# HGRN2's value projection in wide tiles with its heads turned on VectorE, the start and the layers' seams in another order: a four-layer decoder trunk on one core

## The chip, the core and the metric

One Trainium2 chip, one of its cores. The metric is device time in microseconds (us) of one execution. PE is TensorE, with PEld its weight loads; DVE is VectorE, ACT ScalarE, POOL GpSimd, and SP the engine whose queue issues nearly all DMAs here. The whole trunk runs as one program.

## What is computed

x is 1024 positions by 1024 channels in fp32. Four layers follow one another: HGRN2, sliding-window attention (SWA), gated DeltaNet (GDN), HGRN2 again.

```python
for i in range(DEPTH):                                  # 4
    mod = (c @ ada_w[i] + ada_b[i])[:, None, :]
    shift, scale, gate = jnp.split(mod, 3, axis=-1)
    h = rmsnorm(x, norm_g[i]) * (1.0 + scale) + shift
    y = mixer_i(h, ...)                                 # i % 3: 0 HGRN2, 1 SWA, 2 GDN
    x = x + gate * y

def hgrn2_mixer(h, w_in, w_out, onorm_g, lb):           # 8 heads, dk = dv = 128, chunks of 64
    q, f_pre, i_, z = jnp.split(h @ w_in, 4, axis=-1)   # w_in 1024 x 4096
    log_f = jnp.log(lb + (1.0 - lb) * jax.nn.sigmoid(f_pre))
    k = (1.0 - lb) * jax.nn.sigmoid(-f_pre)
    o = hgrn2_scan(silu(q), k, i_, log_f)               # S = exp(b_last) S + k^T v, o = A v + q exp(b) S
    return (rmsnorm(o, onorm_g) * jax.nn.silu(z)) @ w_out
```

SWA has 16 query heads over 4 key heads of width 64, rotary angles and a norm of q and k, a window of 128. GDN has 8 key heads and 16 value heads of width 128, a short convolution on q, k and v, and a triangular solve per chunk of 64.

## The kernel before

**Layout.** Positions are cut into two halves of HT = 512 (`hf`), each of NC = 4 groups of 128; channels into KT = 8 groups of 128. x is kept with channels on partitions, one SBUF slot per half (`xslot`, two). The normed input of a layer is kept as a pair `hhi`, `hlo` in fp32r (`hslot`, four), every weight as `w_hi`, `w_lo`; a product is `mm3`, three matmuls hi·hi, lo·hi, hi·lo, one PSUM tile over eight channel groups (24 matmuls). `load_w` (L170-186) brings a piece of weights by DMA, rounds it on ACT and takes the remainder on DVE; three raw and four rounded pieces are held.

**Kinds of projection.** `proj_fm` has weights standing and 512 positions streaming (PSUM tile `proj_ps`); `proj_tm` has positions standing and 256 weight columns streaming (`projt_ps`); HGRN2's values, two heads at a time, and all of SWA's q, k and v use `proj_tm`.

**The mixers.** In HGRN2, `mix` takes one head, half by half: products inside blocks of 32 at three levels (`lev_ps`, L1040, and L1087 for the last one, of 96, 64 and 32 columns on three column groups of PE), the transposed keys (`kh_ps`), the output and state matmuls (`o_ps`, `s_ps`), the norm of the output (L1132), its transpose on PE (`ot_ps`, L1136), the gate's multiply on DVE (L1139), and a store to `od` in DRAM (L1141), from where the output projection reads it (`out_load`, `out_mm`; PSUM tile `outp_ps`). Head 7 skips the store. Values lie in `hg_v`, three buffers. In GDN, `conv` empties a projection's PSUM tile on ACT (L644, L648), sums the taps on DVE (L650); `inverse` solves the triangular systems with groups of tiny matmuls (`z_ps`); `scan` carries the state. Outputs of GDN are turned by a transpose of 32x32 blocks on DVE (L859) and four stores.

**What sets the order.** `weave` draws from several generators (a head's mixing, the next heads' projections, the next layer's conditioning `side`) by their yielded costs, and a scheduler places each engine's instructions by priority (`high_priority`); then every engine, and SP's queue too, runs its own list strictly in that order. `tied` keeps a group of matmuls together. A layer's first projections are drawn early (`early`), beside the end of the one before.

**The seams.** After each half of a layer is added to x, `norm` takes the statistics and `norm_apply` writes hhi and hlo of the next layer, eight pieces, each of DVE (L504), ACT (L505), DVE (L506). For SWA and GDN x is spilled to `xd` in DRAM, as its slots are needed.

**The start.** x comes in eight tiles and is transposed on PE; `ada_first` builds the first layer's shift and scale, four parts of 2 MB of `ada_w`, all as rows on PE (`ada_row`, L400), then turned into columns (`ada_ps`, L449). `AO` lists the order of these and of two preloaded weight columns. The first projection follows.

Of the kernel before, what the change touches and what calls it, by code (L numbers as in the profile page):

```python
# [20 lines left out]
P = 128  # L21
T = 1024
# [8 lines left out]
NB = {"n_acc": 1, "n_sq": 2, "n_t": 2}  # L31
# [4 lines left out]
EO, EW, EV = 60, 150, 300  # L36
# [8 lines left out]
AO = ((2, True), (0, True), 0, D, (3, True), (1, True))  # L45

ZL = ((2, 0, 1),), ((3, 0, 1),), ((4, 0, 1),), ((5, 0, 1),), ((6, 0),), ((6, 1),), ((7, 0, 1),), ()
# [36 lines left out]
class Trunk:  # L84
    def __init__(self, ctx, tc, ins):
# [11 lines left out]
        self.od = [self.dram.tile([D * (1 + n), T], F32, name=f"od{n}") for n in range(2)]  # L97
        self.zd = self.dram.tile([2 * D, T], F32, name="zd")
        self.hhi, self.hlo = [None, None], [None, None]
        self.x = [None, None]  # L100
        self.oo, self.pre = {}, {}
# [12 lines left out]
    def early(self, g, pe=0):  # L114

        self.pw, self.pe = EW, pe
        with self.tc.high_priority(offset=EO):
            drain(g)
        self.pw = self.pe = 0
# [25 lines left out]

    def psum(self, tag, name, bufs):
        return self.ps.tile([P, HT], F32, name=name, tag=tag, bufs=bufs)
# [18 lines left out]
    def load_w(self, src, scale=None):  # L166

        nc = self.nc
        shape = list(src.shape)
        raw = self.wp.tile([P, HT], F32, name="w_raw", tag="raw", bufs=RAW)  # L170
        hi = self.wp.tile([P, HT], F32R, name="w_hi", tag="whi", bufs=WB)
        lo = self.wp.tile([P, HT], F32R, name="w_lo", tag="wlo", bufs=WB)
# [22 lines left out]

    def preload(self, w, cols):

        w = w.rearrange("(k p) n -> p k n", p=P)
        self.pre.update((c0, self.load_cols(w, c0)) for c0 in cols)

    def mm3(self, out, a, b, start, stop):
# [4 lines left out]
        mm(out, a[1], b[0], start=False, stop=stop)  # L206
# [87 lines left out]
    def load_x(self, sp, hf):  # L294

        nc = self.nc
        x = self.ins["x"].rearrange("o t d -> (o t) d")
# [3 lines left out]
        for c in range(NC):  # L301
            tt, ts = hf * NC + c, slice(c * P, (c + 1) * P)
            xt = sp.tile([P, D], F32, name="x_in", tag="x_in", bufs=3)
            nc.sync.dma_start(xt, x[tt * P:(tt + 1) * P, :])
            sq = sp.tile([P, D], F32, name="x_sq", tag="x_sq", bufs=1)
            nc.scalar.activation(sq, xt, AF.Square, accum_out=ssq[:, c:c + 1])
            for g in range(2):
# [5 lines left out]
                (nc.scalar.copy if n % 2 else nc.vector.tensor_copy)(dst, src)  # L313
# [3 lines left out]
    def store_x(self, out, hf):  # L317

        nc = self.nc
        o = out.rearrange("o t d -> (o t) d")  # L320
        with self.tc.tile_pool(name=f"out{hf}", bufs=1, reuse_waits="tile", side="right") as op:
            for g in range(2):
                for c in range(NC):
                    t0 = (hf * NC + c) * P
                    xo = op.tile([P, HT], F32, name="x_out", tag="x_out", bufs=5)
                    pt = self.proj_ps("xo_ps")
                    for k in range(4):
                        nc.tensor.transpose(pt[:, k * P:(k + 1) * P], self.x[hf][:, 4 * g + k, c * P:(c + 1) * P], self.ident)
                    (nc.scalar.copy if c % 2 else nc.vector.tensor_copy)(xo, pt)
                    nc.sync.dma_start(o[t0:t0 + P, g * HT:(g + 1) * HT], xo)  # L330
# [57 lines left out]
    def ada_first(self, i, sp, steps):  # L388

        nc = self.nc  # L390
        w = self.ins["ada_w"][i].rearrange("(k p) n -> p k n", p=P)
        for part, pe in steps:
            wk = self.hslot("ada_w0").bitcast(F32)
            for g in range(2):
                nc.sync.dma_start(wk[:, 4 * g:4 * g + 4, :], w[:, 4 * g:4 * g + 4, part * HT:(part + 1) * HT])
            acc = sp.tile([P, HT], F32, name="ada_acc", tag="acc", bufs=2)
            if pe:
                pr = self.psum("lev", "ada_row", 2)
                for k in range(KT):
                    nc.tensor.matmul(pr[0:1, :], self.cT[:, k:k + 1], wk[:, k, :], start=k == 0, stop=k == KT - 1)  # L400
                acc = acc[0:1, :]
                nc.scalar.copy(acc, pr[0:1, :])
            else:
                for k in range(KT):
                    self.ada_step(acc, wk[:, k, :], k)
            self.ada_cols(i, part, acc)
# [59 lines left out]
    def norm(self, i, hf):  # L466
        self.norm_apply(i, hf, self.norm_stats(hf))

# [27 lines left out]
    def norm_apply(self, i, hf, rb):  # L496
        nc = self.nc
# [3 lines left out]
        for k in range(KT):  # L501
            t = self.np.tile([P, HT], F32, name="n_t", tag="n_t", bufs=NB["n_t"])
            G, S = self.gcol[:, i, k:k + 1], self.shift(i, k)
            nc.vector.scalar_tensor_tensor(t, x[:, k, :], G, rb, ALU.mult, ALU.mult)  # L504
            nc.scalar.activation(hhi[:, k, :], t, AF.Identity, bias=S)  # L505
            nc.vector.scalar_tensor_tensor(hlo[:, k, :], t, S, hhi[:, k, :].bitcast(F32), ALU.add, ALU.subtract)  # L506

# [29 lines left out]
    def gdn(self, i, side):  # L537
# [98 lines left out]
        def conv(dd, hf, ps, ct, out):  # L636
# [7 lines left out]
            nc.scalar.copy(xs[:, 3:], ps)  # L644
# [4 lines left out]
            for j in (2, 1, 0):  # L649
                nc.vector.scalar_tensor_tensor(y, xs[:, j:j + HT], w(j), y, ALU.mult, ALU.add)  # L650
# [81 lines left out]
        def inverse(u, dd):  # L732
# [75 lines left out]
            with self.burst():  # L808
                for g in range(N):
                    for z, p_, b_ in ((za, 0, 1), (zb, 2, 3)):  # L810
                        nc.tensor.matmul(z[R[b_], g, :], uv[R[p_], g, R[b_]], Tc[R[p_], g, :], start=True, stop=True)
# [4 lines left out]
            yield 900  # L816
            za, zb = bank("z_ps", 32), bank("z_ps", 32)
            self.tied([f for g in range(N) for f in (
# [6 lines left out]
            yield 1300  # L825
# [666 lines left out]
```

## Time and profile before

| What | Value |
|---|---|
| Time, median of 3 runs | 2690.08 us (2689.09 to 2697.81) |
| Profiled execution, its own time | 2695.95 us |
| Its span | 2694.2 us, mean granted clock 0.992 |
| First projection's matmul | at 55.11 us |
| HGRN2 of layer 0, SWA, GDN, HGRN2 of layer 3 end | about 630, 1110, 2100, 2690 us |
| Matmuls on PE, as recorded | 18,927 (a matmul with fp32 operands is recorded twice, for its two passes) |

A row of a timeline has the start, the duration, engine, line, operation, tiles (out<-in), shape and count; in brackets the idle time ahead of it and what ended it. PE's durations overlap, since matmuls are pipelined, so steps are read from start to start. A row of waits has who waited on whom, the total in us, how often, and the longest. A row of costly groups has busy us and mean ns of one after the bar. A row of DMA issues has the size of one and the median us from issue to landing.

### The profile page before, as it was taken

The numbers are of one execution on the slowest core, as the hardware profiler recorded it, in microseconds if no ns is written. First come the engines' busy times: TensorE is split into PE (matmuls) and PEld (weight loads), VectorE is DVE, ScalarE is ACT, GpSimd is POOL, SyncE is SP. The second block draws the span as 40 slices with busy tenths as digits, with TensorE's granted clock in tenths as the row PEclk, the third lists the DMA queues.
The fourth block names the chain that finished last, engine by engine and source line by source line (L and its number), as shares of the span: only waits on it lengthen the run. The fifth ranks groups of instructions, "written<-read, shape, count | busy, mean of one in ns | idle before, by whom it ended". The sixth has DMA issues, their size and how long they took to land.

```text
span 2694.2 us, 51458 instructions
## 1 busy us (share of the span) xinstructions
PE 2609.7 (97%) x18927; PEld 2102.4 (78%) x18927; DVE 2010.2 (75%) x5619; ACT 1272.9 (47%) x3268; POOL 136.7 (5%) x352
## 2 busy tenths in 40 slices
PE   8999999999999999999999999999999999999998
PEld 4878878778878777677877777777788878787877
DVE  6776766788687877777988888989876766656575
ACT  4333333444454655454556556666644433333342
POOL 0000100000000000001001101100000000000000
PEclk9999999999999999999999999999999999999999
DMA  6332222344223252333343333333584221111133
GB/s 241 92 93 84 68 79 72 110 137 157 59 87 103 75 158 91 114 98 84 102 115 99 96 105 100 94 97 82 179 254 132 71 60 37 56 51 43 49 118 115
DMA packets 361490, 273.29 MB, mean 101 GB/s; under 512 B 70499, under 2 KB 294166, under 8 KB 361238
## 3 DMA queue, kind: packets, MB, share of 16 engines
q1 hardware_dynamic: 360950, 268.96, 33.9%
q8 instruction: 149, 2.44, 0.4%
q14 instruction: 103, 0.84, 0.1%
q0 software_dynamic: 288, 1.05, 0.1%
HBM read 224.77 MB, written 45.15 MB: 100 GB/s over the span
## 4 chain that ended last, share of the span: by engine, by line
PE 71%; DVE 17%; DMA 5%; ACT 3%; issue 3%; SPq 1%; POOL 0%; DVEq 0%; ACTq 0%; POOLq 0%
PE proj_ps L206 10%; PE proj_ps L205 9%; PE proj_ps L204 9%; PE outp_ps L204 5%; PE outp_ps L205 5%; PE outp_ps L206 5%; DMA ada_w<-in_ada_w_dram 3%; PE projt_ps L204 3%; PE projt_ps L206 3%; PE projt_ps L205 3%; DVE w_lo L180 2%; DVE gd_tb L650 2%; PE pv_ps L1374 1%; DVE ada_acc L413 1%; PE w_ps L890 1%
## 5 line engine op out<-in xcount | busy, mean ns | idle before, releaser
L204 PE MATMUL proj_ps<-hhi,w_hi 128*128 128x512 f32 x1664 | 675.8, 406 | 6.1 <-ACT gd_tb L648 5.9
L206 PE MATMUL proj_ps<-hhi,w_lo 128*128 128x512 f32 x1664 | 679.9, 409 | 0.0
L205 PE MATMUL proj_ps<-hlo,w_hi 128*128 128x512 f32 x1664 | 671.2, 403 | 0.0
L204 PEld LDWEIGHTS proj_ps<-hhi,w_hi 128*128 128x128 f32 x1664 | 315.3, 190 | 59.4 <-ACT gd_tb L648 6.3
L205 PEld LDWEIGHTS proj_ps<-hlo,w_hi 128*128 128x128 f32 x1664 | 314.7, 189 | 59.0 <-issue 2.4
L206 PEld LDWEIGHTS proj_ps<-hhi,w_lo 128*128 128x128 f32 x1664 | 315.0, 189 | 56.1 <-issue 1.0
L179 ACT CAST w_hi<-w_raw 128x512 fp32r<-128x512 f32 x332 | 202.0, 611 | 303.3 <-PE proj_ps L205 188.1
L180 DVE TENSOR_TENSOR w_lo<-w_raw,w_hi 128x512 fp32r<-128x512 f32 x332 | 223.1, 674 | 155.2 <-ACT w_hi L179 129.1
L205 PE MATMUL projt_ps<-w_lo,hhi 128*128 128x256 f32 x896 | 258.7, 291 | 4.7 <-DVE w_lo L180 4.7
L204 PE MATMUL projt_ps<-w_hi,hhi 128*128 128x256 f32 x896 | 257.8, 290 | 0.6 <-ACT w_hi L179 0.6
L206 PE MATMUL projt_ps<-w_hi,hlo 128*128 128x256 f32 x896 | 256.8, 290 | 0.0
L204 PE MATMUL outp_ps<-o_hi,w_hi 128*128 128x512 f32 x576 | 229.2, 400 | 4.7 <-ACT o_hi L1200 3.4
L205 PE MATMUL outp_ps<-o_lo,w_hi 128*128 128x512 f32 x576 | 229.4, 399 | 0.0
L206 PE MATMUL outp_ps<-o_hi,w_lo 128*128 128x512 f32 x576 | 226.8, 396 | 0.7 <-DVE w_lo L183 0.7
L205 PEld LDWEIGHTS projt_ps<-w_lo,hhi 128*128 128x128 f32 x896 | 171.1, 192 | 8.1 <-DVE w_lo L180 6.0
L204 PEld LDWEIGHTS projt_ps<-w_hi,hhi 128*128 128x128 f32 x896 | 171.1, 192 | 3.7 <-ACT w_hi L179 1.0
L206 PEld LDWEIGHTS projt_ps<-w_hi,hlo 128*128 128x128 f32 x896 | 170.8, 192 | 2.4 <-issue 1.0
L650 DVE SCALAR_TENSOR_TENSOR gd_tb<-gd_xs,taps,gd_tb 128x512 f32<-128x512 f32 x192 | 145.2, 756 | 28.3 <-ACT gd_tb L648 19.7
L182 ACT ACTIVATE w_hi<-w_raw,par 128x512 fp32r<-128x512 f32 (+1 forms) x136 | 94.3, 698 | 137.0 <-PE outp_ps L205 89.2
L204 PEld LDWEIGHTS outp_ps<-o_hi,w_hi 128*128 128x128 f32 x576 | 108.8, 189 | 29.1 <-ACT o_hi L1200 4.9
L413 DVE SCALAR_TENSOR_TENSOR ada_acc<-ada_w,par,ada_acc 128x512 f32<-128x512 f32 x140 | 104.8, 749 | 33.4 <-DMA ada_w<-in_ada_w_dram 32.5
L206 PEld LDWEIGHTS outp_ps<-o_hi,w_lo 128*128 128x128 f32 x576 | 108.7, 189 | 23.5 <-DVE w_lo L183 1.3
(398 smaller groups left out, 4894.8 us busy)
## 6 DMA issues: line engine op xcount, KB each, us to landing
ada_w<-in_ada_w_dram SPq DMA_DIRECT2D x160, 256.0 KB, 2.8
w_raw<-in_hg_in_w_dram SPq DMA_DIRECT2D x136, 256.0 KB, 2.8
w_raw<-in_gd_in_w_dram SPq DMA_DIRECT2D x108, 256.0 KB, 3.0
o_in<-od SPq DMA_DIRECT2D x72, 256.0 KB, 3.2
w_raw<-in_gd_out_w_dram SPq DMA_DIRECT2D x64, 256.0 KB, 2.9
w_raw<-in_sw_in_w_dram SPq DMA_DIRECT2D x48, 256.0 KB, 2.9
w_raw<-in_hg_out_w_dram SPq DMA_DIRECT2D x40, 256.0 KB, 2.8
ada_w<-in_ada_w_dram SPq DMA_DIRECT2D x8, 1024.0 KB, 9.2
```

The lines of the kernel that those rows point to most:

```text
L179: nc.scalar.copy(hi, raw)
L180: nc.vector.tensor_tensor(lo, raw, hi.bitcast(F32), ALU.subtract)
L182: nc.scalar.activation(hi, raw, AF.Copy, scale=scale)
L204: mm(out, a[0], b[0], start=start, stop=False)
L205: mm(out, a[0], b[1], start=False, stop=False)
L206: mm(out, a[1], b[0], start=False, stop=stop)
L413: self.nc.vector.scalar_tensor_tensor(acc, w, c, acc, ALU.mult, ALU.add)
L650: nc.vector.scalar_tensor_tensor(y, xs[:, j:j + HT], w(j), y, ALU.mult, ALU.add)
L890: nc.tensor.matmul(po[:, hd[a]], dd["u"][a, hf][:, cs], rhs, start=True, stop=True)
L1374: nc.tensor.matmul(po[a * 64:(a + 1) * 64], vg[:, n + 1 - nkb + b, :], p4[:, :, a, :], start=b == 0, stop=b == nkb - 1)
```

## The change

It has eight parts; the names are those of the code after.

1. *Wide values.* HGRN2's values are projected 512 columns at a time (`proj_wide`, PSUM tile `projw_ps`), four heads at once, over all eight groups of positions. They lie in the two slots of x, head 7's apart (`v7`); so x is spilled in HGRN2 layers too, and comes back (`fill_x`) ahead of the output projection. From head 1 on z of a head is projected while it is mixed.
2. *Heads 0 to 6 turned on DVE.* The normed output is transposed in blocks of 32x32 on DVE (L1192), stored in four pieces to a scratch `pd` in DRAM (L1195), read back while the next half is mixed (L1074), multiplied by the gate on DVE (L1075) and stored to `od` (L1076).
3. *The last level* is 16 matmuls of 32, 64, 64 and 32 columns on four column groups, tied.
4. *GDN.* The z groups are issued behind the last product (`apart`) and their yields are larger; two more units' gate projections are drawn early.
5. *Norm.* `norm_apply` is a generator, its scratch is in PSUM (`n_t` in the "lev" banks); the second half is drawn inside the next layer, in GDN within `conv`, behind the tap sums (`self.last`, `hold`, `piece`).
6. *SWA.* V and Q are projected first, K after them, with one rsqrt per two tiles; the matmuls of P·V are tied.
7. *Start.* All of `ada_w` is asked for at once, behind half of x; parts 2 and 3 are rows on PE, parts 0 and 1 sums on DVE; the second half of x is copied on ACT alone; tables of angles and taps come last.
8. *The store* of x uses a free slot of hhi instead of a pool of its own.

```diff
+    def apart(self, mms):
+        with self.tc.issue_after(self.mm.ins):
+            self.tied(mms)
...
+        row(2)
+        steps(0)
+        row(3)
+        self.ada_cols(i, 0, acc[0])
+        steps(1)
+        self.ada_cols(i, 1, acc[1])
...
-            t = self.np.tile([P, HT], F32, name="n_t", tag="n_t", bufs=NB["n_t"])
+            t = self.psum("lev", "n_t", 2)
...
-            nc.scalar.copy(xs[:, 3:], ps)
+            with self.tc.issue_after(self.hold.ins) if self.hold else nullcontext():
+                nc.scalar.copy(xs[:, 3:], ps)
...
+            self.piece = None
+            with self.tc.issue_after(last.ins):
+                drain(take(self.last, self.parts))
+            self.hold = self.piece
...
-        self.early(proj_kq(0, ds[0], ((0,),)), EV)
+        self.parts = 4
+        self.early(chain(proj_kq(0, ds[0], ((0,),)), proj_z(1, ds[1], (0,)), proj_z(2, ds[2], (0,))), EV)
+        drain(self.last)
...
+        def gate():
+            h, hf, z = pend.pop()
+            rows = (slice(h * P, (h + 1) * P), slice(hf * HT, (hf + 1) * HT))
+            t = tl("tmp")
+            nc.sync.dma_start(t, self.pd[rows])
+            nc.vector.tensor_tensor(v4(z, "c b"), v4(t, "b c"), v4(z, "c b"), ALU.mult)
+            nc.sync.dma_start(od[rows], z)
...
+                        self.tied([lambda c=c, m=m: mm(c, *m) for c in range(NC) for m in (
+                            (0, 3, slice(6, 7), slice(3, 4)), (0, 0, slice(0, 4, 3), slice(1, 3)),
+                            (1, 1, slice(1, 5, 3), slice(2, 4)), (2, 2, slice(2, 3), slice(3, 4)))])
...
+                    if l == 3 and pend:
+                        gate()
...
                 if h < HA:
-                    nc.sync.dma_start(od[h * P:(h + 1) * P, hf * HT:(hf + 1) * HT], of)
+                    nc.vector.tensor_tensor(v4(on, "b c"), v4(po, "c b"), r[:, :, None, None].to_broadcast([P, NC, 4, 32]), ALU.mult)
+                    ob = tl("tmp")
+                    nc.vector.transpose(ob, on)
+                    dst = self.pd[h * P:(h + 1) * P, hf * HT:(hf + 1) * HT].rearrange("(b q) (a t) -> a q b t", b=4, a=4)
+                    for a in range(4):
+                        nc.sync.dma_start(dst[a], ob[a * 32:(a + 1) * 32].rearrange("q (b t) -> q b t", b=4))
+                    pend.append((h, hf, d["zs", hf]))
...
+        self.spill_x(1)
...
         drain(side)
+        for hf in range(2):
+            self.fill_x(hf)
...
+    def proj_wide(self, ws, evac, tts):
+        for tt in tts:
+            ps = self.proj_ps("projw_ps")
+            hf, ts = tt // 4, slice((tt % 4) * P, (tt % 4 + 1) * P)
+            for k in range(KT):
+                self.mm3(ps, (self.hhi[hf][:, k, ts], self.hlo[hf][:, k, ts]), ws[k], k == 0, k == KT - 1)
...
-        self.early(kv(0))
+        self.early(chain(proj_v(0), proj_q(0, ds[0], (0, 1))))
         self.spill_x(1)
-        drain(kv(1))
-        ds = [dict() for _ in range(G)]
-        drain(proj(0, ds[0]))
+        drain(proj_v(1))
+        drain(self.proj_tm(self.load_tm(w_in, 1024), ev_k))
+        drain(chain(proj_z(0, ds[0]), proj_q(0, ds[0], (2, 3))))
```

How it moves instructions, at three places. First PE at the start, before and after (x_ps: transposes of x; ada_row: row sums of the conditioning; ada_ps: a row or a sum turned into columns; n_rb: the norm's statistics spread over partitions).

```order
L310 MATMUL x_ps<-ident,x_in 128x128 x8
L400 MATMUL ada_row<-ada_w_297,par 1x512 x5
L493 MATMUL n_rb<-n_sq,ones 128x512
L449 MATMUL ada_ps<-ones,ada_acc 128x1 x4
L400 MATMUL ada_row<-ada_w_318,par 1x512 x7
L400 MATMUL ada_row<-ada_w_362,par 1x512 x7
L400 MATMUL ada_row<-ada_w_383,par 1x512 x7
L310 MATMUL x_ps<-ident,x_in 128x128 x23
L265 MATMUL taps_ps<-ident,taps_in 128x128
L204 MATMUL proj_ps<-hhi,w_hi 128x512
```
```order
L326 MATMUL x_ps<-ident,x_in 128x128 x32
L423 MATMUL ada_row<-ada_w_144,par 1x512 x3
L520 MATMUL n_rb<-n_sq,ones 128x512
L423 MATMUL ada_row<-ada_w_144,par 1x512 x5
L479 MATMUL ada_ps<-ones,ada_acc 128x1 x4
L423 MATMUL ada_row<-ada_w_150,par 1x512 x8
L479 MATMUL ada_ps<-ones,ada_acc 128x1 x8
L326 MATMUL x_ps<-ident,x_in 128x128 x4
L326 MATMUL x_ps<-ident,x_in 128x128 x28
L213 MATMUL proj_ps<-hhi,w_hi 128x512
```

Two of the four row sums have left PE; the transposes of x's second half and the columns of the last part still stand ahead of the first projection.

Second ACT at the start of GDN (hhi: a piece of the norm's second half; gd_xs and gd_tb: a projection's PSUM tile emptied by `conv`; w_hi: weights rounded).

```order
L179 CAST w_hi<-w_raw 128x512
L505 ACTIVATE hhi<-n_t,mod 128x512 x2
L644 COPY gd_xs<-proj_ps 128x512
L648 ACTIVATE gd_tb<-proj_ps,taps 128x512
L651 ACTIVATE gd_tb<-gd_tb 128x512
L678 COPY gd_kt<-ktr_ps 128x512
```
```order
L184 CAST w_hi<-w_raw 128x512
L674 COPY gd_xs<-proj_ps 128x512
L678 ACTIVATE gd_tb<-proj_ps,taps 128x512
L686 ACTIVATE gd_tb<-gd_tb 128x512
L533 ACTIVATE hhi<-n_t,mod 128x512 x2
L621 ACTIVATE gd_tmp<-gd_tmp 128x16
L713 COPY gd_kt<-ktr_ps 128x512
```

The first tile is emptied ahead of all eight pieces of the norm's second half, where it stood behind them.

Third SP's queue in the heads of layer 0 (ada_w: the next layer's conditioning; w_raw: weights).

```order
L427 DMA ada_w<-in_ada_w_dram 128x512 x3
L1141 DMA od_76<-hg_tmp 128x512
L427 DMA ada_w<-in_ada_w_dram 128x512 x2
L177 DMA w_raw<-in_hg_in_w_dram 128x4x128 x2
```
```order
L457 DMA ada_w<-in_ada_w_dram 128x512
L1195 DMA pd<-hg_tmp 32x4x128 x4
L457 DMA ada_w<-in_ada_w_dram 128x512 x3
L1074 DMA hg_tmp<-pd 128x512
L457 DMA ada_w<-in_ada_w_dram 128x512
L182 DMA w_raw<-in_hg_in_w_dram 128x4x128 x2
L1076 DMA od_76<-hg_zs 128x512
```

One store per half-head has become four, a reload and a store, with the weight loads between and behind them.

More of the change, by code (lines that the diff above doesn't have):

```diff
@@ L205, in mm3 @@
         mm(out, a[0], b[1], start=False, stop=False)
[L206 removed]
+        self.mm = mm(out, a[1], b[0], start=False, stop=stop)
     def setup(self, tmp):
@@ L320, in store_x @@
         o = out.rearrange("o t d -> (o t) d")
[L321 to L330, printed above, removed]
+        for g in range(2):
+            xs = self.hslot("x_out").bitcast(F32)
+            for c in range(NC):
+                t0 = (hf * NC + c) * P
+                xo = xs[:, c, :]
+                pt = self.proj_ps("xo_ps")
+                for k in range(4):
+                    nc.tensor.transpose(pt[:, k * P:(k + 1) * P], self.x[hf][:, 4 * g + k, c * P:(c + 1) * P], self.ident)
+                (nc.scalar.copy if c % 2 else nc.vector.tensor_copy)(xo, pt)
+                nc.sync.dma_start(o[t0:t0 + P, g * HT:(g + 1) * HT], xo)
     def rope_tables(self, sp):
@@ L807, in inverse @@
             za, zb = bank("z_ps", 32), bank("z_ps", 32)
[L808 to L811, printed above, removed]
+            self.apart([lambda g=g, z=z, p_=p_, b_=b_: nc.tensor.matmul(z[R[b_], g, :], uv[R[p_], g, R[b_]], Tc[R[p_], g, :], start=True, stop=True)
+                        for g in range(N) for z, p_, b_ in ((za, 0, 1), (zb, 2, 3))])
             nc.scalar.copy(Z[R[1], :, 0:32], za[R[1]])
```

288 lines of the change are left out of this document (157 added, 131 removed).

## The prediction

> **What bounds the kernel now.** I read the page first (busy shares, then the chain that ended last), then the table by windows, then the list of PE's waits, and last the timeline of PE where one kind of matmul follows another. From the page:
>
> ```profile
> span 2694.2 us, 51458 instructions
> PE 2609.7 (97%) x18927; PEld 2102.4 (78%) x18927; DVE 2010.2 (75%) x5619; ACT 1272.9 (47%) x3268; POOL 136.7 (5%) x352
> PE 71%; DVE 17%; DMA 5%; ACT 3%; issue 3%; SPq 1%; POOL 0%; DVEq 0%; ACTq 0%; POOLq 0%
> ```
>
> PE is occupied 97% of the span and carries 71% of the chain: the time is the sum of PE's start-to-start steps plus a few waits. By stretch (busy time of PE, PEld, DVE, ACT, POOL, then clock, DMA share):
>
> ```profile
> 67.00:500.00 433.00, 422.44 (x3907) 352.45 (x3906) 297.60 (x932) 150.30 (x366) 27.31 (x56) 1.00 0.29 84
> 630.00:700.00 70.00, 64.01 (x490) 60.56 (x491) 54.89 (x141) 28.27 (x54) 0.00 (x0) 0.98 0.44 144
> 700.00:1090.00 390.00, 380.87 (x2388) 300.45 (x2387) 302.90 (x864) 212.10 (x535) 0.00 (x0) 1.00 0.31 96
> 1260.00:1920.00 660.00, 647.60 (x4623) 518.35 (x4622) 577.14 (x1653) 405.68 (x1283) 56.90 (x138) 0.99 0.38 100
> ```
>
> HGRN2 heads of layer 0 (first row): DVE 297.6/433 = 69%, so DVE has room there. In the gated DeltaNet (last row) DVE is at 87% and PE still at 98%. The seam from HGRN2 to attention (second row) is thin: PE 91%. The longest of PE's waits (total us, times, longest):
>
> ```profile
> PE lev_ps L1040 <- DVE hg_X L1063: 6.8, 19, 1.8
> PE z_ps L828 <- DVE gd_uq L823: 6.6, 7, 1.6
> PE proj_ps L204 <- ACT gd_tb L648: 5.9, 1, 5.9
> PE ot_ps L1136 <- DVE hg_tmp L1132: 5.6, 11, 1.3
> PE projt_ps L205 <- DVE w_lo L180: 4.7, 5, 1.4
> ```
>
> **Prices of PE's steps.** Timeline rows (start, duration as modelled; I use differences of starts only), first a 512-column and a 256-column stream, then interruptions of each:
>
> ```profile
> 2490.21 0.39 PE L204 MATMUL proj_ps<-hhi,w_hi 128*128 128x512 f32 x1
> ...
> 2491.34 0.39 PE L206 MATMUL proj_ps<-hhi,w_lo 128*128 128x512 f32 x1
> ...
> 2511.60 0.28 PE L204 MATMUL projt_ps<-w_hi,hhi 128*128 128x256 f32 x1
> ...
> 2512.91 0.28 PE L206 MATMUL projt_ps<-w_hi,hlo 128*128 128x256 f32 x1
> ```
> ```profile
> 1644.82 0.39 PE L206 MATMUL proj_ps<-hhi,w_lo 128*128 128x512 f32 x1
> 1645.08 0.66 PE L658 MATMUL qtr_ps<-ident,gd_q 128*128 128x128 f32 x4
> 1645.49 0.48 PE L204 MATMUL proj_ps<-hhi,w_hi 128*128 128x512 f32 x1
> 1645.81 0.39 PE L205 MATMUL proj_ps<-hlo,w_hi 128*128 128x512 f32 x1
> ...
> 2504.08 0.52 PE L1040 MATMUL lev_ps<-hg_q,hg_k 128*32 128x48 f32 x32
> 2504.53 0.39 PE L205 MATMUL projt_ps<-w_lo,hhi 128*128 128x256 f32 x1
> ...
> 2508.83 0.28 PE L205 MATMUL projt_ps<-w_lo,hhi 128*128 128x256 f32 x1
> 2509.04 0.85 PE L1087 MATMUL lev_ps<-hg_X,hg_kg 128*32 128x96 f32 x24
> 2509.81 0.39 PE L206 MATMUL projt_ps<-w_hi,hlo 128*128 128x256 f32 x1
> ...
> 2511.28 0.36 PE L205 MATMUL projt_ps<-w_lo,hhi 128*128 128x256 f32 x1
> 2511.49 0.28 PE L206 MATMUL projt_ps<-w_hi,hlo 128*128 128x256 f32 x1
> ```
>
> A 512 step is 1.13/5 = 0.226 us, a 256 step 1.31/11 = 0.119. Four transposes take 1645.49 − 1645.08 = 0.41. Leaving a 256 stream costs 0.21 instead of 0.119, returning 0.21 again: 0.18 us per interruption (0.16 as the median over the 236 such places of this trace). Leaving a 512 stream costs 0.26 for 0.226 and returning 0.32: 0.13 (0.10 as the median over its 792).
>
> **The change, part by part.** Minus is a gain.
>
> 1. *Wide values.* 1,536 matmuls of 256 columns in the two HGRN2 layers become 768 of 512: 768·0.226 − 1,536·0.119 = **−9**. The Trainium skill ("TensorE: Matmul & The Clock Gate", Back-to-back issue gap) has columns over 2.4 plus 2.5 ns for the isolated gap, 215.8 and 109.2 ns, by which the pair would save 2.6 ns and this term would be −2, not −9. The rows disagree with it at both widths (0.226, 0.119).
> 2. *Interruptions.* By the two programs' PE order, the 256 streams are left 236 times before and 129 after, the 512 streams 792 and 808: −107·0.16 + 16·0.10 = **−16**.
> 3. *Transposes of the output.* Heads 0 to 6 lose L1136: 112 transposes, 28 groups of 0.41: **−11**. Their wait on DVE in the list (5.6 us, 28 of 32 groups) goes too: **−5**.
> 4. *Last level.* L1087's 24 records (12 matmuls, two passes) take 0.77 with the return; 32 passes of 48 columns on four column groups take 0.45. The groups run side by side, so the longest decides: 96 columns before, 64 after. Between the two rows 64 columns give 0.45 + 16/48·0.32 = 0.56; 32 half-heads · −0.21 = **−7**.
> 5. *Start.* Rows (L413 from the page):
>
> ```profile
> 27.10 7.03 PE L400 MATMUL ada_row<-ada_w,par 128*1 128x512 f32 x16
> 35.04 7.03 PE L400 MATMUL ada_row<-ada_w,par 128*1 128x512 f32 x16
> 42.97 6.17 PE L400 MATMUL ada_row<-ada_w,par 128*1 128x512 f32 x14
> 55.11 0.50 PE L204 MATMUL proj_ps<-hhi,w_hi 128*128 128x512 f32 x1
> L413 DVE SCALAR_TENSOR_TENSOR ada_acc<-ada_w,par,ada_acc 128x512 f32<-128x512 f32 x140 | 104.8, 749 | 33.4 <-DMA ada_w<-in_ada_w_dram 32.5
> ```
>
>    Row sums stand one behind another on PE until 49. Two of the four go to DVE (8·0.75 = 6 us each) beside the rest. If only PE counted, that is −14; but the loads, DVE's sums, the norm's pieces and the copies of x's second half, now all on ACT and ahead of the first projection on PE, follow in series. Between −14 and +2 I take **−8**: first projection near 47.
> 6. *Seam to attention.* 630–700 at the 98% of the next row would hold 4.4 us more work. V and Q now come first and K's rotations later, so w_lo is less often behind DVE: **−5** (0 to −7; +4 if the norm's second half, now deferred past the seam, delays the projection that reads it).
> 7. *Seam to the gated DeltaNet.* The 5.9 us wait has this cause on ACT, and a slow clock after it:
>
> ```profile
> 1134.82 1.38 ACT L505 ACTIVATE hhi<-n_t,mod 128x512 fp32r<-128x512 f32 x2 [1.07 <-DVE n_t L504]
> 1136.10 0.57 ACT L644 COPY gd_xs<-proj_ps 128x512 f32<-128x512 f32 x1
> ...
> 1137.90 0.63 PE L205 MATMUL proj_ps<-hlo,w_hi 128*128 128x512 f32 x1
> ...
> 1138.33 0.63 PE L206 MATMUL proj_ps<-hhi,w_lo 128*128 128x512 f32 x1
> ```
>
>    The evacuation stood behind the norm's second half; steps of 0.43 instead of 0.226 follow for about nine matmuls (−2). Now the pieces come after the convolution's sums and two gate projections fill PE: 5.9 + 2 = 8, I take **−7**.
> 8. *z groups.* Issued behind a finished product, with wider spacing: of the 6.6 us, **−4** (−6.6 to +3, since 16 tied matmuls still wait in one place).
> 9. *What the new path costs.* Rows:
>
> ```profile
> L859 DVE STREAM_TRANSPOSE gd_of<-gd_of 128x512 f32<-128x512 f32 x32 | 22.5, 704 | 0.1
> x<-xd SPq DMA_DIRECT2D x4, 2048.0 KB, 8.4
> od<-gd_of SPq DMA_DIRECT2D x128, 64.0 KB, 1.8
> od<-hg_tmp SPq DMA_DIRECT2D x28, 256.0 KB, 2.9
> ```
>
>    DVE gets 28·0.70 = 20 us more, 10 in a stretch with 135 us idle. Each half-head's output goes out in four 64 KB pieces (1.8), comes back (about 2.9, by the 256 KB row) and is gated: 1.8 + 2.9 + issue ≈ 6 us. In half of the cases only some nine DVE instructions (about 5 us) stand between transpose and gate, so DVE stands for a us or two, and SP, which issues in order, holds weight loads behind a reload. Nothing to 0.8 us of PE per half-head: 0 to +22. Each layer's x comes back in two transfers of 8.4, covered by about 84 matmuls (19 us): 0 to +8. The norm's scratch in the level banks, and waits such as L1040's 6.8 that lose cover when PE runs faster, lie in the same range. I take **+12**, nearer to the low end, since the gated DeltaNet runs PE at 98% beside an 87% DVE.
>
> Store, rope tables and taps: nothing, all beside projections; if that cover failed, 2 us. Sum: −9 −16 −11 −5 −7 −8 −5 −7 −4 +12 = −60. The profiled execution took 2695.95 (its span 2694.2 and 1.75 around it), so 2636; it stands 5.9 above the median of 2690.08, from which the same sum gives **2630**, my forecast. Less than 0.3% (8 us) either way can't be told from no change here.
>
> **Rivals.**
> - *Waits stay, only counted work goes.* Terms 1 to 4 without the wait are −43, the start gives half (−4), seams and z groups nothing, the new path +10: −37, **2653**. For it: 6 to 8 move waits rather than work, and the next late thing at each seam is the same norm. Against: the 5.9 us has one cause, which the change moves.
> - *A wide step worth two narrow ones.* If the wide products step at 0.236 instead of 0.226, twice a 256 less 2 ns, because their weights or evacuations are tighter, term 1 is 768·0.236 − 183 = −2 and the time **2637**. The 512 stream above stands against it. The gap rule of the Trainium skill ("TensorE: Matmul & The Clock Gate", Back-to-back issue gap) would give the same −2.
> - *Slower: the gate multiply holds DVE.* Write, reload and gate are serial on two in-order engines, 28 times. It decides when PE loses over 72/28 = 2.6 us per half-head, beyond what the w buffers cover (four tiles of 24 matmuls, 22 us). With the full 6 us lost each time: −72 + 168 = +96, **2786**; with 3.5 us +26, **2716**. For it: short distances in DVE's order, and SP waits in order. Against: DVE idle 31% there.
> - *All seams close and the new path is free.* Without +12 and with terms 5, 6 and 8 at their ends (−6, −2, −3 more): **2607**.
>
> **How the numbers follow.** Forecast 0.52 (2615 to 2645 around 2630), waits stay 0.23, wide step 0.06, all closed 0.12, slower 0.07. The range 2601 to 2662 leaves out the slower case and the far ends of the second and the last, some 0.2 in all. Faster: 0.52 + 0.23 + 0.06 + 0.12 = 0.93, less 0.01 for what ends within 0.3%; the slower case gives 0.06 and another 0.01 within: 0.92, 0.02, 0.06.
>
> **What would show it.** The first projection near 47 us; no ot_ps groups except head 7's; last-level groups of about 0.56 to the next matmul; no 6 us wait at the start of the gated DeltaNet; PE's share in layer 0's heads still 96% or more. I am wrong if DVE idles before the gate multiply on a reload for over 40 us in all while PE waits for DVE, if PE waits for x's transfers ahead of the output projection, or if the seams show new waits as long as the old.

## The result: slower, and the profile after

The changed kernel takes 2710.55 us (median of 6 runs, 2706.75 to 2718.79) against 2689.59 for the kernel before (6 runs): ratio 1.0076, 95% interval 1.0058 to 1.0093. Forecast were 2630 us and a range of 2601 to 2662. The sign was wrong.

The page of the changed kernel, its line on the span, the one on the engines, and the chain:

```profile
span 2715.0 us, 50592 instructions
PE 2583.8 (95%) x18271; PEld 2059.4 (76%) x18271; DVE 2031.2 (75%) x5661; ACT 1282.7 (47%) x3342; POOL 150.3 (6%) x352
PE 69%; DVE 15%; DMA 7%; ACT 4%; issue 3%; POOL 1%; SPq 1%; DVEq 0%; ACTq 0%; POOLq 0%
```

The span less PE's busy time is 84.5 us before (2694.2 − 2609.7) and 131.2 after: 47 us more in which PE stands. The mean granted clock was 0.992 before and is 0.979 now. A slow clock costs time only while PE has work, so I add up the stretches at half clock in each trace (before, then after; length, then busy PE, PEld, DVE, ACT, POOL):

```profile
sum 44.25, PE 37.97 PEld 29.63 DVE 29.74 ACT 20.25 POOL 3.33; mean PE 3.80 PEld 2.96 DVE 2.97 ACT 2.03 POOL 0.33
sum 113.26, PE 82.89 PEld 64.69 DVE 69.64 ACT 40.89 POOL 7.02; mean PE 4.36 PEld 3.40 DVE 3.67 ACT 2.15 POOL 0.37
```

Half of PE's busy time in them, 19 us before and 41 after, is the estimated loss to the slow clock: 22 more. What is left of the busy time, 2590.7 before and 2542.3 after, fell by 48 us. So work was taken off PE, and 69 us of standing and slow clock came in its place. Where, the list of PE's waits says (total us, times, longest):

```profile
PE o_ps L1171 <- POOL hg_at L1134: 12.8, 8, 2.1
PE vtr_ps L693 <- DVE gd_tb L687: 12.6, 9, 7.2
PE projw_ps L213 <- ACT w_hi L184: 11.3, 1, 11.3
PE z_ps L843 <- ACT gd_Tc L828: 5.9, 1, 5.9
PE proj_ps L215 <- DVE w_lo L185: 4.8, 3, 2.2
PE projw_ps L214 <- DVE w_lo L185: 4.4, 2, 4.2
PE outp_ps L215 <- DVE w_lo L188: 4.4, 2, 3.2
PE lev_ps L1093 <- DVE hg_X L1116: 4.2, 13, 0.7
```

The first four make 42.6 us. What answers to them in the list of before is 1.4 us of vtr_ps for DVE and 0.6 of the narrow projt_ps for w_hi. The same places in the table by windows, for before (first three rows) and after (last three): behind the first projections, at the end of the gated DeltaNet's projections, and the heads of layer 3. After the window and its length come busy PE, PEld, DVE, ACT, POOL, the clock, DMA's share.

```profile
63.00:83.00 20.00, 19.86 (x228) 18.34 (x227) 19.40 (x48) 10.77 (x19) 0.00 (x0) 1.00 0.14 41
1911.00:1941.00 30.00, 26.11 (x150) 19.95 (x147) 22.11 (x45) 20.58 (x63) 0.00 (x0) 0.94 0.51 154
2146.00:2582.00 436.00, 429.78 (x4108) 357.54 (x4095) 272.96 (x939) 157.00 (x378) 29.37 (x64) 1.00 0.16 49
```
```profile
63.00:83.00 20.00, 4.52 (x12) 3.01 (x11) 16.50 (x38) 10.34 (x17) 2.21 (x4) 0.57 0.28 100
1911.00:1941.00 30.00, 14.84 (x247) 12.33 (x247) 15.34 (x34) 9.91 (x26) 3.61 (x6) 0.60 0.71 206
2163.00:2604.00 441.00, 424.17 (x3850) 335.14 (x3849) 271.95 (x950) 154.85 (x398) 45.42 (x64) 0.98 0.23 71
```

In the first window PE works 4.5 of 20 us, with DVE busy 16.5; in the second 14.8 of 30, at a clock of 0.60. In layer 3's heads PE is busy 5.6 us less, and they take 5 us longer.

**Place 1, at 63 us.** PE (two rows) waits for the second of the eight weight pieces that one wide product needs. ACT (six rows) makes it at 73.94, behind the norm's second half and the sines of the angle tables. Then PE waits again, for the piece's remainder from DVE; DVE's own row (the last) names the store of an angle table as what it waited for:

```profile
74.59 0.79 PE L213 MATMUL projw_ps<-w_hi,hhi 128*128 128x512 f32 x1 [11.25 <-ACT w_hi L184]
79.61 0.80 PE L214 MATMUL projw_ps<-w_lo,hhi 128*128 128x512 f32 x1 [4.22 <-DVE w_lo L185]
```
```profile
65.85 0.61 ACT L184 CAST w_hi<-w_raw 128x512 fp32r<-128x512 f32 x1
66.36 0.69 ACT L533 ACTIVATE hhi<-n_t,mod 128x512 fp32r<-128x512 f32 x1
68.70 1.35 ACT L533 ACTIVATE hhi<-n_t,mod 128x512 fp32r<-128x512 f32 x2 [1.65 <-DVE n_t L532]
70.07 1.28 ACT L383 ACT_TABLE_LOAD   x1
73.31 0.42 ACT L383 ACTIVATE rope_ang<-rope_ang 128x256 f32<-128x256 f32 x1 [1.96 <-DVE rope_ang L382]
73.94 0.60 ACT L184 CAST w_hi<-w_raw 128x512 fp32r<-128x512 f32 x1
78.86 0.69 DVE L185 TENSOR_TENSOR w_lo<-w_raw,w_hi 128x512 fp32r<-128x512 f32 x1 [1.93 <-DMA rope_sw_qnorm<-cg_sw_qnorm]
```

**Place 2, at 1911 us.** The last convolution has no projection beside it any more, so its whole chain over ACT and DVE shows. The last unit's triangular solve follows, and PE waits again: for ACT, whose row names a transfer as what held it. This second hole is the z_ps wait of 5.9 in the list:

```profile
1910.60 0.48 PE L215 MATMUL proj_ps<-hhi,w_lo 128*128 128x512 f32 x1
1918.26 1.11 PE L693 MATMUL vtr_ps<-ident,gd_tb 128*128 128x128 f32 x4 [7.18 <-DVE gd_tb L687]
1924.58 0.65 ACT L828 COPY gd_Tc<-gd_tmp 128x512 f32<-128x512 f32 x1 [4.02 <-DMA od<-gd_of]
1925.28 1.92 PE L843 MATMUL z_ps<-gd_Tc,gd_uq 32*32 32x32 f32 x64 [5.90 <-ACT gd_Tc L828]
```

**Place 3, in layer 3, head after head.** POOL copies the diagonal blocks (four copies, L1134); PE's o_ps waits for them:

```profile
2394.15 0.73 POOL L1134 COPY hg_at<-hg_A 32x128 f32<-32x128 f32 x1 [76.00 <-DVE hg_A L1129]
2395.46 3.78 POOL L1134 COPY hg_at<-hg_A 32x128 f32<-32x128 f32 x2
2399.29 0.49 PE L1171 MATMUL o_ps<-hg_v,hg_at 128*128 128x128 f32 x2 [1.78 <-POOL hg_at L1134]
```

The two copies of the second row take 3.78 us, against 0.47 for one on the mean before. All three places come with slow clock. Windows of the changed kernel, cut to the stretches at half clock that go with the three waits:

```profile
65.60:82.70 17.10, 3.88 (x8) 2.77 (x9) 13.60 (x33) 9.06 (x15) 2.21 (x4) 0.50 0.27 97
1915.60:1939.50 23.90, 13.26 (x239) 11.14 (x240) 11.22 (x17) 6.34 (x13) 3.61 (x6) 0.50 0.68 196
2400.30:2403.70 3.40, 3.40 (x45) 2.78 (x47) 1.65 (x7) 0.86 (x3) 0.00 (x0) 0.50 0.20 61
```

The first two stretches begin while PE still waits (it stopped at 63.34 and at 1911.08), so their length overlaps the waits, and only PE's 3.88 and 13.26 busy us in them run slower. In the last row PE is busy for the whole stretch and still gets half the clock: 1.7 us lost behind a wait of 1.8.

### The profile page after: what moved, and what is told of

Read it like the earlier page. It is cut to its first block, busy times and chain, and to the rows that moved or that the text cites. A ratio compares the mean times of both kernels' runs of the same rounds, so it can differ in the third digit from the quotient of the medians.

```text
span 2715.0 us, 50592 instructions
## 1 busy us (share of the span) xinstructions
PE 2583.8 (95%) x18271; PEld 2059.4 (76%) x18271; DVE 2031.2 (75%) x5661; ACT 1282.7 (47%) x3342; POOL 150.3 (6%) x352
## 4 chain that ended last, share of the span: by engine, by line
PE 69%; DVE 15%; DMA 7%; ACT 4%; issue 3%; POOL 1%; SPq 1%; DVEq 0%; ACTq 0%; POOLq 0%
PE proj_ps L213 9%; PE proj_ps L215 9%; PE proj_ps L214 9%; PE outp_ps L214 5%; PE outp_ps L213 5%; PE outp_ps L215 5%; DMA ada_w<-in_ada_w_dram 2%; PE projw_ps L214 2%; PE projw_ps L215 2%; PE projw_ps L213 2%; DVE gd_tb L680 2%; DVE w_lo L185 1%; POOL hg_at L1134 1%; PE projt_ps L214 1%; PE projt_ps L215 1%
## 5 line engine op out<-in xcount | busy, mean ns | idle before, releaser
L185 DVE TENSOR_TENSOR w_lo<-w_raw,w_hi 128x512 fp32r<-128x512 f32 x356 | 239.0, 675 | 161.4 <-ACT w_hi L184 156.5
L184 ACT CAST w_hi<-w_raw 128x512 fp32r<-128x512 f32 x356 | 217.0, 611 | 278.5 <-PE proj_ps L214 161.2
L443 DVE SCALAR_TENSOR_TENSOR ada_acc<-ada_w,par,ada_acc 128x512 f32<-128x512 f32 x154 | 114.9, 746 | 25.9 <-DMA ada_w<-in_ada_w_dram 24.6
L214 PEld LDWEIGHTS outp_ps<-o_lo,w_hi 128*128 128x128 f32 x576 | 110.7, 192 | 23.8 <-issue 1.4
L1134 POOL COPY hg_at<-hg_A 32x128 f32<-32x128 f32 x128 | 72.2, 564 | 994.6 <-DVE hg_A L1129 511.2
L188 DVE SCALAR_TENSOR_TENSOR w_lo<-w_raw,par,w_hi 128x512 fp32r<-128x512 f32 (+1 forms) x136 | 96.6, 715 | 40.7 <-ACT w_hi L187 39.3
L213 PE MATMUL projw_ps<-w_hi,hhi 128*128 128x512 f32 x256 | 103.0, 405 | 11.3 <-ACT w_hi L184 11.3
L214 PE MATMUL projt_ps<-w_lo,hhi 128*128 128x256 f32 x384 | 110.6, 290 | 2.3 <-DVE w_lo L185 2.3
L213 PE MATMUL projt_ps<-w_hi,hhi 128*128 128x256 f32 x384 | 110.5, 290 | 2.0 <-ACT w_hi L184 2.0
```

The costliest lines, as they stand in the source:

```text
L184: nc.scalar.copy(hi, raw)
L185: nc.vector.tensor_tensor(lo, raw, hi.bitcast(F32), ALU.subtract)
L188: nc.vector.scalar_tensor_tensor(lo, raw, scale, hi.bitcast(F32), ALU.mult, ALU.subtract)
L213: mm(out, a[0], b[0], start=start, stop=False)
L214: mm(out, a[0], b[1], start=False, stop=False)
L443: self.nc.vector.scalar_tensor_tensor(acc, w, c, acc, ALU.mult, ALU.add)
```

## Experiments

The theory: three places, each with its waits and the slow clock at it, hold most of the 69 us. By the windows above, PE's idle time and half of its busy time at half clock give 15.5 + 1.9 = 17 at place 1, 15.2 + 6.6 = 22 at place 2, and at place 3 12.8 + 5·1.7 = 21: some 60, an estimate. (The expectations below count one wait and half of the whole slow stretch, 11.3 + 8.5 and 7.2 + 12. That comes near by luck: it takes the overlap twice and leaves out the second wait at each place.) The rival: the waits are symptoms, and whatever one place wins the next takes. Runs on different chips are compared by their ratio to the kernel before, the changed kernel's being 1.0076; 0.001 is 2.7 us.

**Copies on ACT.**

```diff
-    nc.gpsimd.tensor_copy(at[gs, :, gs], A[gs].rearrange(...))
+    nc.scalar.copy(at[gs, :, gs], A[gs].rearrange(...))
```

> The changed kernel with one line moved: the four 32x128 copies of a half-head's diagonal blocks (hg_at, L1134) run on ACT instead of POOL. Theory (the fourth copy on POOL takes 3.26 us instead of 0.46 while DVE runs operations back to back, PE waits 12.8 us for it in 8 places, and each wait is followed by 3.4 us at half clock): the waits of o_ps on hg_at and the half-clock stretches of layer 3's heads go, 12.8 + 5 x 1.7 = 21, of which some 18 are won: about 2692 us. Rival (the copies only change queue: they then stand behind ACT's other work and o_ps waits for ACT): 2705 to 2712 us, with a wait of o_ps on ACT in the list.

2695.77 us, ratio 1.0013 (1.0004 to 1.0023): −17 us by the ratios. Its heads of layer 3, by window, which stood at 441 us:

```profile
2160.00:2583.00 423.00, 415.63 (x3849) 328.99 (x3847) 267.24 (x949) 172.90 (x462) 0.00 (x0) 1.00 0.24 74
```

They are 18 us shorter, the clock is whole again, and no wait of o_ps on hg_at is among the longest. The theory holds.

**Why the copies are slow: two runs.** In the first, k's scaling moves from DVE to ACT; in the second it stays on DVE and gets a second SBUF input.

```diff
-    nc.vector.tensor_scalar(k0, k0, om, None, ALU.mult)
+    nc.scalar.activation(k0, k0, AF.Copy, scale=om)                       # first
+    nc.vector.tensor_tensor(k0, k0, om.to_broadcast([P, HT]), ALU.mult)   # second
```

> The changed kernel with the copies left on POOL, but layer 3's scaling of k (L1020, a TENSOR_SCALAR on DVE of 0.47 us during which each slow copy starts) done on ACT. Theory A (the one-input TENSOR_SCALAR locks POOL out and it stays out until DVE pauses): no copy over 1 us in layer 3, about 2697 us. Theory B (any unbroken run of DVE operations with two SBUF inputs keeps POOL out, as in layer 0 where no TENSOR_SCALAR precedes the one slow copy): copies of 2 to 3.3 us stay, 2705 to 2712 us.

> The changed kernel with the copies on POOL, and layer 3's scaling of k (L1020) left on DVE but written with two SBUF inputs (TENSOR_TENSOR against the factor spread along the row, about 0.68 us instead of 0.47). Theory A (what locks POOL out is the one-input TENSOR_SCALAR): no copy over 1 us in layer 3, time near that of the variant with this operation on ACT, about 2700 us. Theory B (the unbroken run of large two-input operations that follows keeps POOL out, whatever stands at its head): copies of 2.3 us or more stay in layer 3, 2706 to 2714 us.

First: 2702.2 us, 1.0039 (1.0026 to 1.0053), the slow copies of layer 3 are gone (two of 2.8 and 1.1 us in layer 0 are left). Alone this reads as theory A. Second: 2712.93 us, 1.0075 (1.0058 to 1.0091), and five of layer 3's six are back, longer, without any TENSOR_SCALAR. Minimum, median and maximum in ns of the copies, in the second:

```profile
L1134 POOL COPY hg_at<-hg_A x128: 279/372/3466, 93.3 to 2605.6; 32x128 f32<-32x128 f32 x128
```

So theory A falls. In both kernels the slow copies of layer 3 began 0.12 us into the first of a row of DVE operations of 0.4 us and more, one behind another without a pause, were held for six to eight of them, and ended some 0.15 us behind one. But theory B, as it was put, doesn't hold either. Two copies of the second run, each begun just as far into L1020, with the first DVE operations of the same row:

```profile
2397.83 3.47 POOL L1134 COPY hg_at<-hg_A 32x128 f32<-32x128 f32 x1
2397.71 0.68 DVE L1020 TENSOR_TENSOR hg_k<-hg_k,omlb 128x512 f32<-128x512 f32 x1
2398.32 0.55 DVE L1152 TENSOR_TENSOR hg_kg<-hg_kg,hg_F 128x384 f32<-128x384 f32 x1
2398.78 0.41 DVE L1024 TENSOR_TENSOR hg_kg<-hg_k,hg_f 128x256 f32<-128x256 f32 x1
```
```profile
2260.45 0.71 POOL L1134 COPY hg_at<-hg_A 32x128 f32<-32x128 f32 x1
2260.34 0.68 DVE L1020 TENSOR_TENSOR hg_k<-hg_k,omlb 128x512 f32<-128x512 f32 x1
2260.94 0.64 DVE L1152 TENSOR_TENSOR hg_kg<-hg_kg,hg_F 128x384 f32<-128x384 f32 x1
2261.50 0.51 DVE L1024 TENSOR_TENSOR hg_kg<-hg_k,hg_f 128x256 f32<-128x256 f32 x1
```

One is held for 3.47 us; the other gets through in 0.71, and the DVE operations behind it are 0.1 us longer. In the first run too, the last copies of layer 3's half-heads begin in such rows, and most take 0.45. What lets a copy in between two operations of a row stays open. The cure doesn't hang on it, since the copies on ACT leave POOL.

**Angle tables early.**

```diff
+    k.rope_tables(sp)
     k.ada_first(layers[0], sp, wks)
...
     k.conv_taps(sp)
-    k.rope_tables(sp)
```

> The changed kernel with the angle tables computed ahead of the conditioning's sums again, as in the kernel before, instead of last. Theory (at 63 us PE waits 11.3 us for the second piece of the values' weights, because ACT and DVE have the norm's second half and the angle tables ahead of it; 17.1 us at half clock follow, 8.5 lost): the wait falls below 5 us and the slow stretch with it, -12 to -17: about 2696 us; the first projection comes 1 to 3 us later. Rival (three raw buffers and SP's order hold the loads back, not ACT and DVE): a wait of 8 us or more stays, 2705 to 2712 us.

2698.75 us, 1.0024 (1.0015 to 1.0034): −14. The wait at 63 us is gone; one of 0.56 is what is left at this product:

```profile
70.77 0.73 PE L213 MATMUL projw_ps<-w_hi,hhi 128*128 128x512 f32 x2 [0.56 <-ACT w_hi L184]
```

The price is a first projection at 53.1 us instead of 48.5, 4.6 us later where 1 to 3 were expected: 14 won and 4.6 paid make 19, near the 17 estimated for this place. SP's buffers were not the cause.

**Gate projections of the gated DeltaNet as before.**

```diff
-ZL = ((2, 1), (3, 0)), ((3, 1), (4, 0)), ((4, 1), (5, 0)), ((5, 1), (6, 0)), ((6, 1),), ((7, 0),), ((7, 1),), ()
+ZL = ((2, 0, 1),), ((3, 0, 1),), ((4, 0, 1),), ((5, 0, 1),), ((6, 0),), ((6, 1),), ((7, 0, 1),), ()
...
-    self.early(chain(proj_kq(0, ds[0], ((0,),)), proj_z(1, ds[1], (0,)), proj_z(2, ds[2], (0,))), EV)
+    self.early(proj_kq(0, ds[0], ((0,),)), EV)
...
-    (chain(proj_z(0, ds[0], (1,)), proj_v(0, ds[0]), proj_z(1, ds[1], (1,)), proj_kq(1, ds[1])), 62400, ...)
+    (chain(proj_z(0, ds[0], (1,)), proj_v(0, ds[0]), proj_z(1, ds[1]), proj_kq(1, ds[1])), 72800, ...)
```

> The changed kernel with the gated DeltaNet's gate projections in the order of before: unit 7's last, none of units 1 and 2 drawn early, 24 weight loads fewer. Theory (the change took the filler of the last unit away: PE waits 7.2 us at 1911 for the last convolution and 23.9 us at half clock follow, 12 lost): that wait goes, -19, and the seam into the layer loses 4 to 8 again for want of filler: about 2698 us. Rival (the wait at 1911 is DVE's order, not missing filler): it stays, and the seam's loss is added, 2714 to 2720 us.

2688.79 us, 0.9992 (0.9981 to 1.0004): −23. Both waits of place 2, 7.2 and 5.9, are gone, and the loss at the seam did not come back. So the change had moved filler (two half units, 10.4 us each by their yields) from where it was missed to where it was not.

**The three together.**

> The changed kernel with three of the edits tried alone: hg_at's copies on ACT, the angle tables ahead of the conditioning's sums, the gated DeltaNet's gate projections in the order of before. Theory (three separate places, each with its wait and its half-clock stretch): the three gains add, -15 -12 -22 = -49 against the changed kernel, about 2661 us, and half-clock time below 50 us. Rival (what one wins, the next wait takes): 2675 to 2686 us.

2663.66 us, 0.9892 (0.9876 to 0.9909): −49 against the changed kernel, where the three alone give −17 −14 −23 = −54. They add, nearly. The clock is 0.989; its stretches at half clock add up to 60 us, where fewer than 50 were expected. The rival falls. From here the change's own steps can be weighed, since PE no longer stands at these places.

**Heads turned on PE again** (on top of the three; transposes on PE, one store, no scratch):

```diff
-    nc.vector.transpose(ob, on)
-    for a in range(4):
-        nc.sync.dma_start(dst[a], ...)
+    for c in range(NC):
+        nc.tensor.transpose(pt[:, cs], on[:, cs], self.ident)
+    nc.vector.tensor_tensor(of, pt, d["zs", hf], ALU.mult)
+    nc.sync.dma_start(od[h * P:(h + 1) * P, hf * HT:(hf + 1) * HT], of)
```

> The kernel with the three edits, and heads 0 to 6 turned by transposes on PE again and stored once, as before (part 2 of the change undone). Theory (112 transposes of 0.10 us, their wait on DVE and the interruptions of the stream are PE's time): 11 + 5 + about 3 more than the three edits alone, some +16 to +19. Rival (the way over DRAM costs as much in DVE's and SP's time as it saves on PE, the 12 us of the prediction's ninth step): 0 to +4.

2674.14 us, 0.993 (0.9914 to 0.9945): +10. PE's busy time rises by 15.7 (2567.0 to 2582.7 on the pages). So the turn on DVE is worth 10 us net, between the two. If PE's 15.7 are all its gain, the way over DRAM costs about a third of it; that cost was not measured by itself.

**The last level in three column groups again** (on top of the three):

```diff
-    self.tied([... 16 matmuls, 32/64/64/32 columns ...])
+    self.tied([lambda c=c, g=g: m3(c, g) for c in range(NC) for g in range(3)])   # 96/64/32
```

> The kernel with the three edits, and the last level as 12 matmuls of 96, 64 and 32 columns on three column groups again (part 3 undone). Theory (groups run side by side and the longest decides, 96 against 64 columns, 0.21 us in 32 half-heads): +7 us, and 0.77 us from its first matmul to the next stream's. Rival (16 matmuls cost as much as 12 longer ones): 0 to -3 us.

2665.01 us, 0.9896 (0.9881 to 0.9911): +1, not to be told from nothing. The size on PE was right: from the first matmul of the changed kernel's group to the next stream's it is 0.58 us, against 0.78 before (first two rows):

```profile
2501.08 0.85 PE L1087 MATMUL lev_ps<-hg_X,hg_kg 128*32 128x96 f32 x24
2501.86 0.39 PE L205 MATMUL projt_ps<-w_lo,hhi 128*128 128x256 f32 x1
```
```profile
2505.88 0.65 PE L1138 MATMUL lev_ps<-hg_X,hg_kg 128*32 128x32 f32 x32
2506.46 0.50 PE L215 MATMUL proj_ps<-hhi,w_lo 128*128 128x512 f32 x1
```

That is 32·0.2 = 6.4 us of PE, of which the time shows none for certain. The two profiled executions have equal spans, 2660.9 us, and PE is busy 2567.0 with the four groups and 2571.6 with three: the time that PE saved, it stood instead. On what it waited instead stays open.

**Norms applied at once** (on top of the three):

```diff
-                if hf == 0:
-                    drain(a)
-                    k.spill_x(0)
-                else:
-                    k.last = a
+                drain(a)
```

> The kernel with the three edits, and each norm's second half applied at once at the end of the layer before, as before (the deferral of part 5 undone). Theory (the tile's evacuation stood behind the norm's second half on ACT; the deferral took that wait away): the wait of some 6 us at the first projections of the gated DeltaNet and its slow clock come back, +6 to +10. Rival (other priorities at the seam keep it away, or the deferral costs elsewhere what it wins there): -3 to +3.

2659.92 us, 0.9877 (0.9862 to 0.9891): −4, with overlapping intervals. The 6 us wait of before does not come back, and ACT still empties the tile ahead of the norm's second half, without the deferral:

```profile
1102.75 0.59 ACT L674 COPY gd_xs<-proj_ps 128x512 f32<-128x512 f32 x1 [2.29 <-PE proj_ps L215]
1107.53 0.69 ACT L533 ACTIVATE hhi<-n_t,mod 128x512 fp32r<-128x512 f32 x1 [3.60 <-DVE n_t L532]
```

So the order on ACT that was credited is there, but deferring the second half is not what makes it; what else at that seam does was not isolated.

**Narrow values** (on the last kernel; products of 256 columns, the storage in x's slots kept):

```diff
-            yield from self.proj_wide(self.load_wide(w_in, 2 * D + m * HT, mp), ev, range(2 * NC))
+            for hf in range(2):
+                for pr in range(2):
+                    yield from self.proj_tm(wss[pr], ev, (2 * hf, 2 * hf + 1))
```

> The kernel of the last run (three edits, norms applied at once), with HGRN2's values projected 256 columns at a time again, still into the two slots of x (the matmul shape of part 1 undone, its storage kept). Theory (rows of before: 768 x 0.226 against 1536 x 0.119, and by PE's order 58 more interruptions of 256 streams at 0.16, 63 fewer of 512 streams at 0.10): 9 + 3 = +12 us against it, about 2672. Rival (a wide step is worth two narrow ones less 2 ns): +2 to +5. Second rival (narrow evacuations and the shorter span per weight piece free ACT and DVE at the start): 0 or a gain.

2669.12 us, 0.9915 (0.99 to 0.993): +10 by the ratios. That the wide product pays is shown; that its step pays 9 is not. Wide steps inside their stream in the changed kernel:

```profile
2347.93 0.39 PE L213 MATMUL projw_ps<-w_hi,hhi 128*128 128x512 f32 x1
...
2349.32 0.39 PE L213 MATMUL projw_ps<-w_hi,hhi 128*128 128x512 f32 x1
```

1.39/6 = 0.232 us, which is also the median of its 693 undisturbed steps at full clock; a narrow one has a median of 0.120. So the shape gives 1,536·0.120 − 768·0.232 = 6 us. With the 3 of the interruptions that is 9, near the 10 measured. How the 10 divide stays uncertain: the mean clock of this run's executions is 0.987, against 0.989 without the edit.

**Angle tables first of all** (on the same kernel, called ahead of the conditioning's loads).

> The same kernel of the last run, with the angle tables computed ahead of everything of the conditioning, their three small loads ahead of its 8 MB in SP's queue. Theory (with the loads behind the 8 MB the tables start at 33.8 us and push the first projection to 52.7; DVE stood idle from 25 to 30 us): first projection near 48 us, -3 to -6: about 2655. Rival (the tables only delay the conditioning's sums): first projection at 52 or later, -1 to +2.

2662.38 us, 0.9891 (0.9877 to 0.9906): +4, overlapping, so no gain. First projection at 52.2: the rival. DVE's idle stretch was not what held the start.

**The z groups as before** (on the same kernel: `tied` for `apart`, yields and weights of before).

> The same kernel of the last run, with the z groups issued and paced as before (part 4's apart, its yields and weights undone). Theory (the prediction's eighth step: PE waited 6.6 us for DVE ahead of the groups, and the change takes two thirds away): +3 to +6. Rival (PE waits elsewhere in the same stretch, DVE being at 87%): -2 to +2.

2657.25 us, 0.9873 (0.9857 to 0.989): −1, the rival. This is the lowest ratio measured, 1.3% under the kernel before, not to be told from the kernel with the norms applied at once. It keeps the wide values, the heads turned on DVE, the last level, the loads of the start and the order of SWA.

A kernel with the norm's scratch back in SBUF was not tried.

## Why the prediction was wrong, step by step

The step that failed is the sum's silence on new waits. It took the waits of before, priced their going, and allowed 12 us for the new path, 2 for tables and taps if their cover failed, and 2 for slow clock. The runs show three new places at which PE stands, worth 14, 23 and 17 us when undone one by one and 49 together.

- *What bounds it* was read rightly, PE's steps and a few waits, and the waits' sum was taken for a small correction. Standing moved by +47, and the slow clock by an estimated +22.
- *1, wide values, −9:* the sign and the size in time are right (10 measured), in part by luck: the changed kernel's step is 0.232, between the 0.226 of the forecast and the 0.236 of the rival, which makes the term 6, and interruptions have a share in the 10. The Trainium skill's gap rule ("TensorE: Matmul & The Clock Gate", Back-to-back issue gap) would have made it −2, by 2.6 ns a pair; the rows have 2·0.120 − 0.232 = 0.008 us, so they decide against it and against the forecast's 12 ns.
- *2 and 3, interruptions and transposes, −16 −11 −5:* the transposes' part held on PE (15.7 busy us come back with them) and was 10 in time. The interruptions were not tried by themselves. The 48 us that left PE stand against 9 + 16 + 11 + 7 = 43 counted and 14 for the start's two row sums: 57, so some of these terms were too large.
- *4, last level, −7:* right on PE (6.4), not shown in the time (1, error about 4).
- *5, start, −8:* the first projection came at 48.5, near the 47 forecast. The failure is the step's end. It stopped at the first projection and did not ask what the next product needs, which stood behind the norm and the angle tables on ACT and DVE. "Store, rope tables and taps: nothing, all beside projections" is the sentence that failed: 14 us, where 2 were allowed.
- *7, seam to the gated DeltaNet, −7:* the wait went, but not by the deferral or the two gate projections that were credited, since without either it stays away. These two were taken from the last units. I named the work that came in and not the place that it left: 23 us.
- *6, −5:* waits moved. At the seam to attention the w_lo wait of 4.7 became 2.3, and 4.4 stand at the output projection. What the time gained there was not tested.
- *8, z groups, −4:* the 6.6 us wait on DVE fell to 3.0, but the old pacing is as fast. The 5.9 us that the z groups wait in one place are place 2's second hole, gone when the fillers are back.
- *9, the new path, +12:* the rival that was feared, DVE held by the reload ahead of the gate's multiply, did not happen: that wait is 3.0 us in all, twice. What did happen in these heads, POOL's copies held up beside DVE, was on no list: 17 us.
- *Slow clock:* two us were allowed for it at one seam. The three places have some 17 us of it, by half of PE's busy time in their slow stretches.

By its number the rival "slower", 2716, comes nearest to the 2711 measured, and that is luck: its mechanism is the wait that stayed at 3.0 us. By mechanism the nearest is "waits stay, only counted work goes", 2653, and it too counted the waits of before as if none could be added. Even without the three places the kernel gains 29 us, not 60. Undone singly, the wide values were worth 10, the turn 10, the last level 1, the z groups' pacing and the deferral nothing, and the first projection comes 2 us earlier, not 8 (52.8 against 55.1).

## What to carry to other kernels

When a kernel runs its main engine at 97%, count twice for every piece of work that is moved: what it covers where it goes, and what it covered where it stood. Follow a reordered start or seam past its first product, to the second and third thing that this engine will ask for, with all that stands ahead of it on the other queues. A change that mixes several edits can hide a gain of nearly 2% behind three local waits; taking them one at a time, by the list of waits, found it.

## What the runs showed of the hardware

A wait of PE can cost more than its length. Behind five waits of 1.8 to 2.1 us in the changed kernel's layer 3 came 3.4 us at half clock each, with PE busy throughout. It is not so every time: behind four such waits of 1.78 us in layer 3, the run with early angle tables has one slow stretch and the run with the old gate projections two. The longer waits, 11.3 and 7.2 us, had half clock from 2.2 and 4.5 us after PE stopped, for 17.1 and 23.9 us in all; PE was busy for only 3.88 and 13.26 us of these, so most of that slow time cost nothing more. The Trainium skill ("TensorE: Matmul & The Clock Gate", HAM oscillation — how this bites in real kernels) puts the rule as no gaps over about 3.4 us; here half clock followed waits of 1.8 to 2.1 us, five times in layer 3.

A small copy on POOL can take seven times its usual length beside DVE: 3.26 us, and 3.47 with the longer operation, instead of 0.47. The Trainium skill ("Perfetto Trace Analysis", Optimizing Scalar/DVE Operations) says that the two share an SBUF read port, which a DVE operation that uses both ports locks. That this port is what held the copies is a reading that fits the traces, not one that a run isolated. The traces add that a copy was held through up to eight DVE operations, TENSOR_TENSORs alone in one run, and that another begun in the same row got through after the first.
